# Two mixture-of-experts stages on Trainium2: the conditional blocks for overflowing tokens, two long ones per stage or six short ones

## The chip, the cores and the metric

The kernel runs on one core of one Trainium2 chip. The metric is the device time of one execution in microseconds (us). A core has five engines, each with its own list of instructions: PE (TensorE, the matrix products), DVE (VectorE), ACT (ScalarE), POOL (GpSimd) and SP (SyncE, which here issues the loads of the weights). An engine's sequencer (PEq, DVEq, ACTq, POOLq in the rows) walks the list, branches, and hands work to the engine; on PE it can be some microseconds ahead of the products. A conditional block is a compare-and-branch in the list of every engine that has work in the block: each reads the tested number into a register of its own and jumps over the block if the test fails.

## What is computed

A transformer of two layers on 256 tokens of width 1024, followed by further mixers and feed-forward stages. Each layer ends in a mixture of 16 experts of hidden width 512 in which every token takes two experts:

```python
D_MODEL = 1024
SEQ = 256
N_EXPERTS = 16
N_GROUPS = 4
TOP_K = 2
D_EXPERT = 512
# per token x and chosen expert e, with the gate weight cs[e]:
#   y += cs[e] * ((silu(x @ exp_w_gate[e]) * (x @ exp_w_up[e])) @ exp_w_down[e])
```

All three expert matrices are f32, 2 MB each, so that one layer's experts are 96 MB. How many tokens choose an expert is known only at run time.

## The kernel before, in words

An expert stage (`moe`, called once in each layer) takes the 16 experts in eight pairs, p = 0 to 7. The two experts of a pair sit side by side in the columns of PE. Each expert has 64 **places**: the tokens that chose it are brought into its places, pass through the three matrices, and are added back to their rows. For one pair PE runs, in this order:

- `up`: 16 rows of products for the gate (`pg`) and 16 for the up matrix (`pu`, both line 1486), out of `hg`, the pair's gathered tokens.
- the scatter that the pair before left over: products `py` (lines 1527 and 1528), whose sum DVE adds to `x` (line 1530); between its two halves stand four transposes `hT` (line 184) of the hidden values, for which ACT's silu and DVE's product are waited for.
- eight transposes `hgT` (line 184), which make the next pair's columns out of rows that POOL gathered (`rows`, line 1426, into the buffers `xh` and `xl`).
- `down`: 16 rows of products `po` (line 1540), whose result becomes `eo`, which is scattered in the next pair.

Where an expert has more than 64 tokens, two conditional blocks serve 32 further places each: `more_up` (line 1680) ahead of `pg`, and `more_down` (line 1683) ahead of `po`, in every pair from the third on. What the places don't hold goes through `rest` (lines 1620 to 1675): a block under `If(left > 96)` (line 1627) that takes all 128 tokens of one half of the sequence through one expert after the other, with its own loads of the weights on POOL's queue into `xh` and `xl`. `rest` stands twice in a stage, in the sixth pair (p = 5, first half of the tokens) and in the seventh (p = 6, second half), between `pu` and the silu; each block holds 16 shares, one for each expert. `left` is the largest count of the stage, with 32 added for the first two pairs, which have no further places. With the given inputs no count goes above 96, so that all engines jump over the block; `more_up` and `more_down` are run in some pairs and jumped over in others.

The weights come in 12 transfers of 1 MB for each pair, issued by SP into a ring of 18 slots: a slot is free again when the products of an earlier pair have read it. The order of instructions on an engine is the order of the code, within which a scheduler can move those that aren't pinned. [...] One row of f32 products in the lists below is four instructions (two weight loads and two products), one transpose is two.

## Time and profile before

| | us |
|---|---|
| median of three runs | 1566.06 |
| lowest and highest of the three | 1565.14 to 1566.18 |
| the profiled execution's own time | 1567.53 |
| its span in the trace | 1565.7 |
| PE busy in it | 1480.8 (95%) |
| DVE busy | 918.6 (59%) |
| ACT busy | 674.0 (43%) |

The span runs from the first to the last instruction of the profiled execution, and that execution's own time is 1.8 us more than its span. All times of the rows are counted from the span's start; the first expert stage lies at about 216 to 444, the second at about 604 to 821. A busy PE says only that a product was under way: a wait for a weight, for a branch or for another engine shows as idle time between products, and it is these that the rows are about.

### The profile page before, as it was taken

To read this page: it belongs to the slowest core of one execution; us is meant where nothing else is said; L and a number is where in the kernel's file an instruction comes from. 1 tells how busy PE (TensorE), PEld (TensorE's weight loads), DVE (VectorE), ACT (ScalarE), POOL (GpSimd) and SP (SyncE) were. 2 spreads that over 40 slices of the span, in tenths; PEclk is the share of its full clock that TensorE was granted. 3 is DMA by queue.
4 is the path that set the end of the run, shared out by engine and by line. 5 is a ranking of instruction groups with operands and counts; after the bars stand their busy time and mean duration, and the time that the engine had idled before them with its cause. 6 is when DMAs were issued, how large, how long until landed. Compare 5 with 4: busy or idle time off the path is not lost. (4 is left out here: it accounts for less than half of the span.)

```text
span 1565.7 us, 22964 instructions
## 1 busy us (share of the span) xinstructions
PE 1480.8 (95%) x8719; PEld 1046.1 (67%) x8719; DVE 918.6 (59%) x1800; ACT 674.0 (43%) x1404; POOL 141.2 (9%) x192
## 2 busy tenths in 40 slices
PE   6999999999989998999888999899999999999998
PEld 3666653334369974343336887788887997788886
DVE  3756453233269975332237867766667786766666
ACT  3444341111145543111016456655556565665554
POOL 0321011000000001000003001200001211110000
PEclk9999999999989999999999999999999999999999
DMA  9998999999967989999987531745463543546540
GB/s 357 335 316 302 348 420 417 421 418 418 376 215 246 318 326 413 419 420 419 418 362 235 159 120 65 239 143 197 163 211 121 182 135 97 193 143 212 190 161 27
DMA packets 172510, 418.13 MB, mean 267 GB/s; under 512 B 10376, under 2 KB 94016, under 8 KB 147792
## 3 DMA queue, kind: packets, MB, share of 16 engines
q1 hardware_dynamic: 165696, 403.46, 69.5%
q0 software_dynamic: 6400, 12.78, 2.5%
q8 instruction: 88, 1.44, 0.4%
q14 instruction: 54, 0.44, 0.1%
q10 hardware_dynamic: 272, 0.00, 0.0%
HBM read 422.13 MB, written 3.19 MB: 272 GB/s over the span
## 5 line engine op out<-in xcount | busy, mean ns | idle before, releaser
L230 DVE TENSOR_TENSOR hl<-w,hl 128x1024 fp32r<-128x1024 f32 x280 | 336.5, 1234 | 51.7 <-ACT hl L229 51.6
L229 ACT CAST hl<-w 128x1024 fp32r<-128x1024 f32 x280 | 280.3, 1046 | 32.0 <-DMA w<-in_even_w_in 19.0
L2350 PE MATMUL pgu<-hT,hl 128*128 128x512 f32 x640 | 224.4, 393 | 0.0
L2351 PE MATMUL pgu<-hT,hl 128*128 128x256 f32 x640 | 178.0, 279 | 0.0
L381 PE MATMUL lin<-hl,hThi 128*128 128x256 f32 (+2 forms) x480 | 159.3, 335 | 2.0 <-ACT hl L229 1.3
L382 PE MATMUL lin<-hl,hThi 128*128 128x256 f32 (+2 forms) x480 | 153.9, 321 | 2.0 <-DVE hl L230 1.7
L383 PE MATMUL lin<-hl,hTlo 128*128 128x256 f32 (+2 forms) x480 | 153.0, 320 | 0.4 <-DVE hTlo L558 0.4
L2350 PEld LDWEIGHTS pgu<-hT,hl 128*128 128x128 f32 x640 | 119.9, 187 | 27.1
L2351 PEld LDWEIGHTS pgu<-hT,hl 128*128 128x128 f32 x640 | 120.5, 188 | 2.0
L1540 PE MATMUL po<-w,hidT 128*64 128x512 f32 x512 | 114.6, 600 | 4.6 <-DVE x L1530 2.1
L1500 DVE TENSOR_TENSOR hd<-hd,pu 128x512 f32<-128x512 f32 x16 | 11.0, 687 | 183.8 <-PE pu L1486 183.8
L1486 PE MATMUL pg<-w,hg 128*64 128x512 f32 x512 | 113.7, 595 | 3.9 <-PEq L1680 3.6
L1486 PE MATMUL pu<-w,hg 128*64 128x512 f32 x512 | 115.0, 593 | 1.1 <-DMA w<-in_exp_w_up 1.1
L381 PEld LDWEIGHTS lin<-hl,hThi 128*128 128x128 f32 x480 | 92.9, 194 | 17.4 <-issue 8.1
L382 PEld LDWEIGHTS lin<-hl,hThi 128*128 128x128 f32 x480 | 92.9, 194 | 11.2 <-DVE hl L230 3.8
L383 PEld LDWEIGHTS lin<-hl,hTlo 128*128 128x128 f32 x480 | 92.6, 193 | 7.8 <-issue 1.7
L1486 PEld LDWEIGHTS pu<-w,hg 128*64 128x64 f32 x512 | 42.3, 137 | 70.8 <-issue 64.3
L1486 PEld LDWEIGHTS pg<-w,hg 128*64 128x64 f32 x512 | 40.1, 137 | 73.6 <-issue 57.7
L1540 PEld LDWEIGHTS po<-w,hidT 128*64 128x64 f32 x512 | 37.6, 138 | 71.4 <-issue 63.3
L1555 ACT CAST eo<-of 128x512 fp32r<-128x512 f32 x32 | 19.8, 618 | 130.4 <-DVE of L1552 130.1
L381 PE MATMUL linc<-hThi,hl 128*128 128x256 f32 x224 | 66.2, 296 | 0.0
L1443 ACT ACTIVATE hg<-hgT,ab 128x128 f32<-128x128 f32 x48 | 18.1, 457 | 111.0 <-PE hgT L184 111.0
(571 smaller groups left out, 2866.2 us busy)
## 6 DMA issues: line engine op xcount, KB each, us to landing
w<-in_exp_w_gate SPq DMA_DIRECT2D x64, 1024.0 KB
w<-in_exp_w_down SPq DMA_DIRECT2D x64, 1024.0 KB
w<-in_exp_w_up SPq DMA_DIRECT2D x64, 1024.0 KB
w<-in_ada_w SPq DMA_DIRECT2D x48, 1024.0 KB
w<-in_ffn_wg SPq DMA_DIRECT2D x22, 1024.0 KB
w<-in_ffn_wu SPq DMA_DIRECT2D x22, 1024.0 KB
w<-in_ffn_wd SPq DMA_DIRECT2D x22, 1024.0 KB
w<-in_even_w_in SPq DMA_DIRECT2D x14, 1024.0 KB
```

The lines of the kernel that those rows point to most:

```text
L229: pin(self.nc.scalar.copy(w[:, 0], src))
L230: pin(self.nc.vector.tensor_tensor(w[:, 1], src, w[:, 0].bitcast(F32), op=ALU.subtract))
L381: pin(mm(out, lh, rh, start=start, stop=False))
L382: pin(mm(out, lh, rl, start=False, stop=False))
L383: pin(mm(out, ll, rh, start=False, stop=stop))
L1443: nc.scalar.activation(out[:, k, :], pt[:, k, :], AF.Identity, scale=self.ab[:, 0, b, k:k + 1], bias=self.ab[:, 1, b, k:k + 1])
L1486: pin(mm(pp[64 * j:64 * j + 64, :], hg[0][:, p % 2, k, 64 * j:64 * j + 64], w[j][k // 4][:, k % 4, :], start=k == 0, stop=k == KD - 1, til ...
L1500: V.tensor_tensor(hd, hd, pu, op=ALU.mult)
L1540: pin(mm(po[c][64 * j:64 * j + 64, :], hidT[:, k, 64 * j:64 * j + 64], W[2][j][k // 2][:, k % 2, 512 * c:512 * c + 512], start=k == 0, sto ...
L1555: nc.scalar.copy(eh[c], of)
L2350: mm(pp[i], wh[:, k, :], both[:, :, k, :], start=k == 0, stop=False)
L2351: mm(pp[i][:, 0, :], wl[:, k, :], hi[:, k, :], start=False, stop=k == KD - 1)
```

## The change

`rest` becomes one block of five or six shares in every pair from the third to the eighth, instead of sixteen shares in each of two pairs: 6, 6, 5, 5, 5 and 5 shares in p = 2 to 7, in the order first half of the tokens, then second half. The number `left` is read into the engines' registers once in a stage and kept, instead of once for each block, and the copy that puts it where it can be read (`count_of(0)`) moves from p = 3 to p = 0. The weights' mask `wv`, the fetch of the half's rows and their columns are made again in each block (twice in the one that holds shares of both halves). In the changed kernel the `If` of `rest` stands on line 1633, its reading on line 1630, `more_up` on 1687 and `more_down` on 1690.

```diff
                 if FIRST <= p + 1 < 8:
                     count_of(p + 1)
-                if p == 3:
+                if p == 0:
                     count_of(0)
...
-            def rest(p, t):
-
-
-                left = nc.values_load(number_of[0][0:1, 0:1], min_val=0, max_val=2 * S,
-                                      engines=engines + (mybir.EngineType.Pool,))
-                with tc.If(left > 96):
+            left = []
+            shares = deque((t, e) for t in range(2) for e in range(NE))
+
+            def rest(p):
+
+
+
+                if not left:
+                    left.append(nc.values_load(number_of[0][0:1, 0:1], min_val=0, max_val=2 * S,
+                                               engines=engines + (mybir.EngineType.Pool,)))
+                mine = [shares.popleft() for _ in range(6 if p < 4 else 5)]
+                with tc.If(left[0] > 96):
...
-                    V.tensor_scalar(wv[:, 0:2 * FIRST], rk[:, t, 0:2 * FIRST], 64.0, None, op0=ALU.is_gt)
-                    V.tensor_scalar(wv[:, 2 * FIRST:], rk[:, t, 2 * FIRST:], 96.0, None, op0=ALU.is_gt)
-                    V.tensor_tensor(wv, wv, cs[:, t, :], op=ALU.mult)
-                    nc.gpsimd.dma_start(space[0][:, 0:D], xd[128 * t:128 * t + 128, 0:D])
-                    columns(space[0][:, 0:D], P, hc, banks[0:2])
...
-                    for e in range(NE):
+                    for q, (t, e) in enumerate(mine):
+                        if q == 0 or t != mine[q - 1][0]:
+                            V.tensor_scalar(wv[:, 0:2 * FIRST], rk[:, t, 0:2 * FIRST], 64.0, None, op0=ALU.is_gt)
+                            V.tensor_scalar(wv[:, 2 * FIRST:], rk[:, t, 2 * FIRST:], 96.0, None, op0=ALU.is_gt)
+                            V.tensor_tensor(wv, wv, cs[:, t, :], op=ALU.mult)
+                            nc.gpsimd.dma_start(space[n % 2][:, 0:D], xd[128 * t:128 * t + 128, 0:D])
+                            columns(space[n % 2][:, 0:D], P, hc, banks[0:2])
...
-                own = up(p, W, (lambda: rest(p, p - 5)) if p in (5, 6) else None)
+                own = up(p, W, lambda: rest(p))
```

The first place is PE's list in the third pair of the first layer (p = 2), as the difference between the two kernels; `be` are the block's own products, `hg` the gathered tokens.

```order
 L1486 MATMUL pg<-w,hg 64x512 x16
 L1486 MATMUL pu<-w,hg 64x512 x16
+L1633 COMPARE_AND_BRANCH
+L184 MATMUL be<-kt,xh 128x128 x8
+L1656 MATMUL be<-xl,hg 128x512 x4
+L1656 MATMUL be<-xh,hg 128x512 x4
...
+L1633 UNCONDITIONAL_BRANCH x2
 L1527 MATMUL py<-eo,kept 128x512
 L1528 MATMUL py<-eo,kept 128x512
```

Where `pu` was followed by the scatter of the pair before, a branch now stands between them, and behind it 6 shares of 24 rows of products and 4 transposes each, which the branch jumps over. In p = 3 to 6 of both layers the branch stands in the same way, right behind `pu`.

The second place is PE's list in the last pair (p = 7) of the first layer, in the changed kernel. Before, `pg` x16, `pu` x16 and the first `py` followed each other there without a branch.

```order
 L1486 MATMUL pg<-w,hg 64x512 x16
 L1486 MATMUL pu<-w,hg 64x512
 L1633 COMPARE_AND_BRANCH
 L184 MATMUL be<-kt,xh 128x128 x8
 L1656 MATMUL be<-xl,hg 128x512 x4
 L1656 MATMUL be<-xh,hg 128x512 x4
...
 L1633 UNCONDITIONAL_BRANCH x2
 L1486 MATMUL pu<-w,hg 64x512 x15
 L1527 MATMUL py<-eo,kept 128x512
 L1528 MATMUL py<-eo,kept 128x512
```

Here the scheduler puts the branch behind the first row of `pu`, and fifteen rows of `pu` come after the jump.

The third place is the first pair (p = 0), as the difference; `ph` are the products that gather the pair's tokens.

```order
 L1380 MATMUL ph<-kept,xh 128x256
 L1380 MATMUL ph<-kept,xl 128x256
+L1630 TENSOR_LOAD cnti_2005
+L1630 ISA x2
 L1486 MATMUL pg<-w,hg 64x512 x8
 L1380 MATMUL ph<-kept,xh 128x256
```

PE's reading of `left` moves from the pairs with a block to a place ahead of the first pair's first product.

## Rows read from the trace of the kernel before

**Rows 1.** Windows: the two stages; span, busy (count) by engine, PEclk, DMA share, GB/s.

```profile
216.00:444.00 228.00, 215.11 (x1075) 90.35 (x1074) 67.86 (x124) 34.24 (x84) 12.12 (x12) 0.98 0.96 395
604.00:821.00 217.00, 202.15 (x959) 86.80 (x958) 63.71 (x117) 31.74 (x75) 13.62 (x14) 0.98 0.99 409
```

**Rows 2.** Timeline, PE, first stage, pairs 4-6: start, duration, what, [idle, releaser].

```profile
345.49 7.07 PE L1486 MATMUL pu<-w,hg 128*64 128x512 f32 x32
...
356.39 7.09 PE L1540 MATMUL po<-w,hidT 128*64 128x512 f32 x32 [0.35 <-DVE x L1530]
...
370.70 7.07 PE L1486 MATMUL pu<-w,hg 128*64 128x512 f32 x32
379.72 0.59 PE L1527 MATMUL py<-eo,kept 128*128 128x512 f32 x1 [1.95 <-PEq L1627]
...
385.62 7.09 PE L1540 MATMUL po<-w,hidT 128*64 128x512 f32 x32 [0.83 <-DVEq L1683]
...
399.90 7.06 PE L1486 MATMUL pu<-w,hg 128*64 128x512 f32 x32
...
412.52 7.09 PE L1540 MATMUL po<-w,hidT 128*64 128x512 f32 x32 [0.34 <-DVE x L1530]
```

**Rows 3.** PE waits, 340 to 440: who for what, us, times, longest.

```profile
PE py L1527 <- PEq L1627: 3.6, 2, 2.0
...
PE po L1540 <- DVEq L1683: 0.8, 1, 0.8
```

**Rows 4.** Timeline of PE, second expert stage, pairs 5 and 6.

```profile
737.98 8.16 PE L1486 MATMUL pu<-w,hg 128*64 128x512 f32 x32
...
754.03 7.09 PE L1540 MATMUL po<-w,hidT 128*64 128x512 f32 x32 [0.30 <-DVEq L1683]
...
773.82 3.65 PE L1486 MATMUL pu<-w,hg 128*64 128x512 f32 x14 [1.05 <-DMA w<-in_exp_w_up]
...
785.79 0.39 PE L1528 MATMUL py<-eo,kept 128*128 128x512 f32 x1 [3.59 <-issue]
...
788.99 7.33 PE L1540 MATMUL po<-w,hidT 128*64 128x512 f32 x32 [0.30 <-DMA w<-in_exp_w_up]
```

**Rows 5.** Waits of PE from 640 to 822.

```profile
PE py L1527 <- PEq L1627: 5.4, 2, 2.8
...
PE pu L1486 <- DMA w<-in_exp_w_up: 1.1, 1, 1.1
```

**Rows 6.** Line 1627: operation, count, ns least/median/most, first, last start.

```profile
L1627 POOLq EVENT_SEMAPHORE  x16: 17/43/7722, 357.2 to 755.2; - x16
...
L1627 POOLq INC_SWDGE_SEM  x4: 746/924/1116, 365.2 to 757.4; - x4
...
L1627 PEldq COMPARE_BRANCH  x4: 5838/5977/6113, 373.3 to 773.9; - x4
```

**Rows 7.** Line 1627 from 372 to 374.

```profile
L1627 PEldq COMPARE_BRANCH  x1: 6102/6102/6102, 373.3 to 373.3; - x1
```

**Rows 8.** Line 1683, whole span.

```profile
L1683 PEldq COMPARE_BRANCH  x13: 71/238/4750, 282.0 to 811.6; - x13
```

**Rows 9.** Line 1680, whole span.

```profile
L1680 PEldq COMPARE_BRANCH  x13: 70/325/2725, 262.4 to 791.9; - x13
```

**Rows 10.** Line 1683 from 380 to 386.

```profile
L1683 PEldq COMPARE_BRANCH  x1: 4750/4750/4750, 380.6 to 380.6; - x1
```

**Rows 11.** DMA queues from 448.5 to 600: packets, MB, share.

```profile
q8 instruction: 9, 0.15, 0.4%
```

**Rows 12.** Windows: stretch of eight of those packets, without a branch.

```profile
448.57:590.45 141.88, 137.49 (x1019) 122.13 (x1019) 123.71 (x204) 81.97 (x154) 7.08 (x9) 0.95 0.83 290
```

**Rows 13.** Page: DMA queues of the whole span.

```profile
q8 instruction: 88, 1.44, 0.4%
```

**Rows 14.** Windows: behind one of PE idle stretches.

```profile
379.90:383.40 3.50, 3.50 (x11) 2.80 (x11) 2.13 (x4) 0.00 (x0) 0.98 (x1) 0.51 1.00 414
```

**Rows 15.** Line 1678: the loads of a count into a register.

```profile
L1678 PEldq TENSOR_LOAD <-cnti x12: 297/302/502, 252.0 to 645.8; - x12
```

## The prediction

> **What bounds the kernel now.** First the windows over the two expert stages [rows 1]: PE is busy for 215.11 of 228 us and for 202.15 of 217, and the DMA share is 0.96 and 0.99. Two resources are near their limit, so the reader has to find out which one ends last, and where. That is read from PE's waits. From 340 to 440 the view has five lines, none of them a transfer; the largest is PE's own sequencer at line 1627, 3.6 us in two waits [rows 3]. In the first stage the weights are there when PE wants them, and whatever PE loses there is lost to the end. From 640 to 822 the largest is the same, 5.4 us in two, but a weight is waited for too, 1.1 us [rows 5], and the `pu` of p = 5 takes 8.16 us [rows 4] where 7.07 is its length in the first stage [rows 2]: there PE has caught up with the transfers, and a loss ahead of that point is first paid out of these two waits, 1.1 + 1.1.

> The jump is partly hidden, because the sequencer is ahead of the products: it begins at 373.3 [rows 7], when `pu` still runs to 377.77 [rows 2], 4.5 us later. Of the 6.1 us, 1.95 show as idle time ahead of the first `py` [rows 2].

> The price of a block is therefore more than that wait. I take the time from the end of `pu` to the start of `po`, which holds the same work in every pair: 3.83 us at p = 4, without a block. With one it is 7.85 at p = 5 and 5.56 at p = 6 [rows 2], in the second stage 7.89 and 11.52 [rows 4]. The prices: 4.0, 1.7, 4.05 and 7.7. [...] Behind the jump of p = 5 the short jump of line 1683 took 4.75 us instead of 0.24 [rows 10], since after landing only the packet at the target is there, and the next one is asked for late. At the last of the four the landing is 18 instructions ahead of a packet's edge, and PE stands a second time, 3.59 us at 785.79 [rows 4]. [...]

> [...]

> **The change part by part.** It removes two far jumps of each stage, 4.0 + 1.7 = 5.7 us in the first and 4.05 + 7.7 = 11.75 in the second.

> It adds six jumps a stage. Five shares are 520 instructions and one half's columns 16, with the semaphore work about 555; with two halves 571, with six shares 659. All are over two packets of 256, so each lands outside of what is held, and costs the sequencer the 5.84 to 6.11 us of the old ones; that a jump is a third as long buys nothing. How much shows depends on where it lands. I counted packet edges in the built list in steps of 256, fixed by the stall at 785.79. With (A) an edge 136 to 147 instructions behind the landing, or right ahead of it, the jump over `more_down`, which itself lands 127 behind, stays in the packet, and only the first stall is left: between 1.7 and 4.05, the prices without a further stall and with half clock; I take 2.9. With (B) the edge 78 to 116 behind, that jump goes into a packet not yet there: 4.0 as at p = 5, bounds 1.7 and 5.1 (plus the weight wait's 1.1). With (C) the edge ten behind: a double stall like 785.79's, 7.7, bounds 6.8 and 8.4, that is 0.8 either way for the clock.

> - First stage: p = 2 is C, p = 3 A, p = 4, 5 and 6 B. At p = 7 the branch stands after one row of `pu`; the sequencer's lead over `pg` is as long as elsewhere, the first stall shows ahead of `pu`'s second row, and the next edge is hidden by fifteen rows (6.6 us): between 1.7 and 3.4, I take 2.5, since no half clock was seen to stretch `pu`. Sum 7.7 + 2.9 + 4.0 x 3 + 2.5 = 25.1, less 5.7: **+19.4**.
> - Second stage: p = 2 and p = 3 are A, p = 4 to 6 B, p = 7 as above: 5.8 + 12.0 + 2.5 = 20.3, less 11.75, less the two weight waits of 2.1 that a later PE no longer meets: **+6.5**.
> - PE's reading of `left` now stands ahead of the first pair's `pg`, behind DVE's copy: 0.30 us in the median of such readings and 0.50 at the longest [rows 15], once in each of two stages. If it falls into the sequencer's lead it costs 0, if all of it shows 1.0; the lead of 4.5 us is there elsewhere, so I take a value near the lower end, **+0.3**. The readings that vanish from the later pairs were in that lead and give nothing.
> - DVE, ACT and POOL jump too; POOL waits for its gathers' landing (7.7 us at the longest) and adds 0.75 to 1.1 [rows 6], now in each pair. Its increments at 365.2 came 8 us ahead of PE's jump at 373.3 [rows 6, 7]: nothing, as long as that lead holds.
> - The weights: no transfer is added while the block isn't taken; a later PE frees slots later, which only matters in the second stage, accounted for above.

> Sum 19.4 + 6.5 + 0.3 = +26.2. The profiled span of 1565.7 becomes about 1592; the profiled execution's own 1567.53 is 1.5 above the median of 1566.06, and the sum is put on the median: **1592**. A measurement of this kernel tells about 0.2%, 3.1 us, from no change.

> **Rivals.**
> (a) The shorter jumps hit what is already held, as a window wider than 660 instructions would have it. Each then costs the 0.24 to 0.33 of the short ones [rows 8, 9], hidden by the lead. The first stage gains 5.7 less six small waits of 0.3, or 3.9; the second, whose `pu` waits for weights already [rows 5], between 0 and 11.75 - 1.8 = 9.9, of which a third is taken, 3.4: about 1559, faster. For it: no jump between 150 and 1,700 instructions is in the trace. Against: a stall at 785.79 at a packet's edge would not be there if more than two were held. [...]
> (b) The jumps cost what I say, and the weights set the time anyway: DMA share 0.96 [rows 1]. Then PE's idle time merges with waits for weights and the sum is 0 to 3: 1566 to 1569. Against: no transfer among the waits of the first stage [rows 3].
> (c) PE's lateness frees slots later, the queue runs dry and a weight is late as well: one more wait of the length of one `pu`, 7.07 [rows 2], with the 1.1 of the weight wait that was there: some 8, about 1600.
> (d) POOL, in every pair now, becomes late: 7.7 + 1.1 = 8.8 us [rows 6] against a lead of 8, about 1 us for which `hgT` waits in each of five pairs of two stages, together 10: about 1602. Against: the 7.7 is the longest of 16, and runs while PE does its products.

> **How the numbers follow.** Forecast 0.66, (a) 0.08, (b) 0.08, (c) 0.10, (d) 0.08. With three A at 1.7 instead of 2.9, both p = 7 hidden and one B per stage at 1.7 the forecast falls by 13, to 1579, and a little below if the clock helps; with A at 4.05, B at 5.1 it rises by 3.5 + 6.6 + 1.8 to 1604, and with (c) or (d) a little more: the range is 1577 to 1608, which leaves out (a), (b) and the tails. Faster is (a), 0.08; same 0.06 and slower 0.02 out of (b), and all the rest slower: 0.86.

> **What would show it.** Six far jumps of 5.8 to 6.1 us in each stage at line 1633; 1.7 to 2.9 us of idle PE ahead of the first `py` in p = 2 to 6 and inside `pu` at p = 7; a second stall at line 1690 in p = 4 to 6; two stalls in p = 2 of the first stage; the first window longer by 19, the second by 6 to 7; no transfer among PE's waits of the second stage. Wrong it would be if the jumps of line 1633 took under a microsecond, or if PE's waits for weights grew by as much as those for its sequencer fell.

## The result and the profile after

The changed kernel takes 1592.58 us in the median of five executions (1589.92 to 1597.39), the kernel before 1566.06 beside it (1564.73 to 1567.34): a ratio of 1.0169, 95% interval 1.015 to 1.0188. It is slower by 26.5 us; 26.2 and 1592 were forecast. The span grew by 22.4 (1565.7 to 1588.1); the profiled execution, 1589.92, is the fastest of the five and lies 2.7 below their median, and that of before lies 1.5 above its own. The rows below are of these two executions and their 22.4 us; the 4.1 us by which the medians differ more stand in no trace.

The windows of the two stages, in the changed kernel, from the first `pg` to the last scatter of each:

```profile
214.30:455.90 241.60, 214.58 (x1073) 95.15 (x1073) 69.02 (x125) 34.34 (x86) 12.03 (x13) 0.98 0.92 375
617.10:843.60 226.50, 205.09 (x958) 88.48 (x958) 61.74 (x112) 30.49 (x73) 12.58 (x13) 0.97 0.95 389
```

Against [rows 1] PE does the same work within longer stretches, and the DMA share has fallen, from 0.96 to 0.92 and from 0.99 to 0.95: the weights are not what PE waits for. Its waits, the longest of the first stage and of the second:

```profile
PE py L1527 <- PEq L1633: 9.3, 5, 2.1
PE hT L184 <- issue: 4.6, 1, 4.6
...
PE po L1540 <- PEq L1690: 2.9, 3, 2.3
```

```profile
PE py L1527 <- PEq L1633: 9.8, 5, 2.1
PE po L1540 <- DMA w<-in_exp_w_up: 6.9, 3, 2.3
...
PE pu L1486 <- PEq L1633: 1.0, 1, 1.0
```

Two waits for its sequencer in a stage have become five, ahead of the first `py`, and in the second stage one more inside the last pair's `pu`. In the first stage the waits of `po` for line 1690 are new; the 6.9 us that the second stage's list puts down to a weight are taken up below. The jumps themselves, by line (1633 is `rest`, 1690 `more_down`):

```profile
L1633 PEldq COMPARE_BRANCH  x12: 3612/6115/6213, 274.8 to 820.3; - x12
```

```profile
L1690 PEldq COMPARE_BRANCH  x13: 82/450/4989, 287.2 to 834.5; - x13
```

Twelve far jumps with a median of 6.1 us, where there were four of 5.98 [rows 6]; one took 3.6. Of the thirteen at line 1690 six took 4.79 to 4.99 us: those of p = 4, 5 and 6 in both stages (4.79, 4.92 and 4.90; 4.99, 4.98 and 4.88). They are the six landings that the prediction had as B, and the seven others took under half a microsecond.

The double stall in p = 2 of the first stage is in PE's timeline:

```profile
272.21 7.07 PE L1486 MATMUL pu<-w,hg 128*64 128x512 f32 x32
281.19 0.48 PE L1527 MATMUL py<-eo,kept 128*128 128x512 f32 x1 [1.91 <-PEq L1633]
...
286.95 1.13 PE L184 MATMUL hT<-kt,hd 128*128 128x128 f32 x4 [4.58 <-issue]
...
291.07 7.09 PE L1540 MATMUL po<-w,hidT 128*64 128x512 f32 x32 [0.30 <-PEq L1690]
```

After the landing four products run, then PE stands again, for 4.58 us, with no releaser named ("issue"), as at 785.79 before [rows 4]. From the end of `pu` to `po` it takes 11.79 us.

That PE's sequencer waits for a fetch at these places can be read from the times of the packets in the queue q8, "instruction" in the view, in the same trace. That PE's list comes through it shows in the kernel before: over the eight packets of [rows 12] the trace has 1019 products, 1019 weight loads and ten semaphore instructions of PE, which gives 256 for each packet of 16 KB. Behind the start of each of the eleven far jumps that took 5.8 us or more the next packet begins after 3.36 to 3.76 us and takes 1.0 to 1.1 us, and the jump ends 1.3 to 1.5 us after it; behind the start of the six long jumps at line 1690 it begins after 2.4 to 2.5 us. At the jump of p = 2 it begins at 278.32; from 278.3 to 279.4 the view of the queues has

```profile
q8 instruction: 1, 0.02, 5.8%
```

The second stall ends in the same way: the packet behind it begins at 284.39 and takes 1.07 us, and PE goes on 1.5 us later, at 286.95. In all fourteen traces together PE has 111 jumps of over 1 us, and each of them ends 1.3 to 1.6 us after the end of such a packet.

One reading has to be made with care. In p = 4 of the second stage the timeline and the list of waits put `po` down to a weight:

```profile
731.89 7.07 PE L1486 MATMUL pu<-w,hg 128*64 128x512 f32 x32
741.02 0.47 PE L1527 MATMUL py<-eo,kept 128*128 128x512 f32 x1 [2.06 <-PEq L1633]
...
743.44 1.11 PE L184 MATMUL hgT<-kt,xh 128*128 128x128 f32 x8
746.89 8.78 PE L1540 MATMUL po<-w,hidT 128*64 128x512 f32 x32 [2.34 <-DMA w<-in_exp_w_up]
```

```profile
L1690 PEldq COMPARE_BRANCH  x1: 4989/4989/4989, 741.6 to 741.6; - x1
```

The sequencer is inside the jump of line 1690 from 741.58 for 4.99 us, to 746.57, and `po` begins at 746.89. The transfer that the view names is one of the up matrix, which `po` does not read, and it has landed only 21.4 us after its issue, at 748.8, when `po` is already running:

```profile
L222 SPq DMA_DIRECT2D w<-in_exp_w_up x1: 328/328/328, 727.4 to 727.4; - x1
...
  PE po L1540: 2.3, 1
...
DMA to landing us min/median/max: 21.4/21.4/21.4
```

The last of the four transfers of the down matrix that `po` does read here landed at 736.3. So the branch is what ended last, not the weight, and the two other waits of this kind, in p = 5 and 6, end in the same way, 0.3 us behind a jump of line 1690. And `po` takes 8.78 us in place of 7.09, at a granted clock of 0.59 from 746.50 to 750.00:

```profile
746.50:750.00 3.50, 3.11 (x8) 1.14 (x10) 0.04 (x1) 0.00 (x0) 0.00 (x0) 0.59 1.04 409
```

### The profile page after: what moved, and what is told of

Its sections match the earlier page's. It is cut to its first block, busy times and chain, and to the rows that moved or that the text cites. A ratio compares the mean times of both kernels' runs of the same rounds, so it can differ in the third digit from the quotient of the medians.

```text
span 1588.1 us, 23110 instructions
## 1 busy us (share of the span) xinstructions
PE 1482.1 (93%) x8719; PEld 1051.2 (66%) x8719; DVE 918.9 (58%) x1800; ACT 673.4 (42%) x1404; POOL 140.7 (9%) x192
## 5 line engine op out<-in xcount | busy, mean ns | idle before, releaser
L1540 PE MATMUL po<-w,hidT 128*64 128x512 f32 x512 | 119.1, 617 | 14.8 <-DMA w<-in_exp_w_up 6.9
L1540 PEld LDWEIGHTS po<-w,hidT 128*64 128x64 f32 x512 | 41.2, 141 | 82.1 <-issue 65.2
L1552 DVE SCALAR_TENSOR_TENSOR of<-po,ws,gate 128x512 f32<-128x512 f32 x32 | 23.9, 748 | 81.8 <-PE po L1540 81.8
```

The lines of the kernel that those rows point to most:

```text
L1540: pin(mm(po[c][64 * j:64 * j + 64, :], hidT[:, k, 64 * j:64 * j + 64], W[2][j][k // 2][:, k % 2, 512 * c:512 * c + 512], start=k == 0, sto ...
L1552: V.scalar_tensor_tensor(of, po[c], ws, gate[:, cs], op0=ALU.mult, op1=ALU.mult)
```

## The experiments

Times are medians; each is compared with executions of the kernel before on the same chip, whose median was 1568.36 us for the kernels with no block, two shares, no products of PE and the early count, 1566.40 for the two splits and the first two early blocks, and 1567.26 for the thin block, the two early blocks with the counts placed, and four shares.

**No block at all.**

```diff
-                own = up(p, W, (lambda: rest(p, p - 5)) if p in (5, 6) else None)
+                own = up(p, W)
```

> The kernel before without either block of rest, so that tokens beyond the places would not be served (there are none with these inputs). Fetch theory (the price of a block is PE's far jump, 5.7 us in the first stage and 11.75 in the second before, of which the second stage's weights give back only a part): 1557 us, 1554 to 1560. If the weights set the time of both stages anyway: 1563 to 1566. Either way this is the floor against which all prices are read.

1561.89 us, ratio 0.9945 (0.9928 to 0.9962): 6.5 us less than before, where 9 were expected; the time lies in neither of the two ranges. The second stage's waits are now for weights:

```profile
PE pu L1486 <- DMA w<-in_exp_w_up: 7.7, 6, 1.3
```

This is the floor: without any jump the first stage is 5.6 us shorter (222.03 against 227.63 from the first `pg` to the last scatter), the second only 1.7 (214.34 against 216.06), since `pu` now waits 7.7 us for weights there, where before it waited 1.1 [rows 5].

**Two shares in a block.**

```diff
-                mine = [shares.popleft() for _ in range(6 if p < 4 else 5)]
+                mine = [shares.popleft() for _ in range(2)]
```

> The changed kernel with two shares in each of the six blocks, 236 instructions of PE instead of 553 to 660; twenty shares are left out. Fetch theory: a jump of less than one packet lands in the packet held or in the next one, already fetched; 1558 us, up to 1566 if one or two lands too early; the jumps under 1 us. Per-block theory (DVE's, ACT's and POOL's jumps, POOL's wait for its gathers, semaphores): as the changed kernel, 1588 to 1595. Length theory (a jump's price in proportion to what it skips): 1571.

1561.41 us, ratio 0.9951 (0.9935 to 0.9967), as the floor.

```profile
L1633 PEldq COMPARE_BRANCH  x12: 313/325/3620, 275.2 to 793.4; - x12
```

Two of the twelve took 3.62 and 1.87 us and show in no wait, the longest at this line being 0.3 us; ten took 0.31 to 0.44. Six conditional blocks whose jump is short cost 2.8 us in the first stage (224.81 against 222.03), and in the second the waits of `pu` for weights are 5.9 us in five, in place of the floor's 7.7 in six.

**Blocks without PE's part, and with a thin one.** In the first a share's products are left out of the code, in the second all but two rows of them and the four transposes, so that the result is not computed; the loads and the work on DVE, ACT and POOL stay. A part of the second's edit:

```diff
-                                for k in range(4):
-                                    mm(banks[2 + i], hc[:, 4 * b + k, :], w[:, k, :], start=b + k == 0, stop=b + k == 4)
+                                if b == 0 and i == 0:
+                                    mm(banks[2], hc[:, 0, :], w[:, 0, :], start=True, stop=True)
...
```

> The changed kernel's six blocks with the same numbers of shares, their loads and their work on DVE, ACT and POOL, but without any product or transpose of PE (a share computes nothing useful), so that PE has nothing to jump over. Fetch theory: 1557 to 1562, no wait of PE at the block's line. Per-block theory: 1585 to 1593, since DVE, ACT and POOL still branch in every pair.

1573.84 us, ratio 1.0042 (1.0027 to 1.0056): neither number. PE's jumps took 0.2 to 0.32 us, but a new wait appeared, here in the first stage:

```profile
PE hT L184 <- DVE hd L1500: 10.5, 6, 2.5
```

With nothing of PE in the block, the scheduler put one of the scatter's adds ahead of it on DVE and another ahead of silu's product, so that `hT` came late. The run can't tell the theories apart, and the thin version, where DVE's order is that of the changed kernel, was made for that:

> The changed kernel's six blocks with all their shares, loads and work on DVE, ACT and POOL, in the changed kernel's order, but with PE's part of a share cut to two rows of products and four transposes (a share computes nothing useful): PE jumps over 107 to 126 instructions in place of 553 to 660. Fetch theory: 1561 us, 1557 to 1566, PE's jumps under 1 us but for one that may meet an edge. Per-block theory (the other engines' jumps and waits): 1585 to 1593. Unlike the block without PE work, the scatter's adds on DVE keep their place behind the block.

1560.75 us, ratio 0.996 (0.9946 to 0.9974), the floor again.

```profile
L1633 PEldq COMPARE_BRANCH  x12: 202/268/418, 275.8 to 793.8; - x12
```

DVE, ACT and POOL branch as often as in the changed kernel, twelve times each at this line, and POOL waits as it does there, 9.1 us at the longest against 8.9; the 32 us between the two kernels hang on how many of PE's instructions the jump passes, 107 to 126 or 553 to 660. This run also has what a block costs without a long jump. From `pu` to `po` it takes 4.18 us in p = 5 of the first stage where 3.85 are the floor, 0.33 more. In the last pair of the first stage, where the block stands inside `pu`, PE pauses although the jump took 0.42 us:

```profile
421.81 1.02 PE L1486 MATMUL pu<-w,hg 128*64 128x512 f32 x2
422.99 7.05 PE L1486 MATMUL pu<-w,hg 128*64 128x512 f32 x30
```

The two products before the block end at 422.83, and the third starts at 422.99 instead of beside them. Behind the block the list has an event on line 1633 that waits for PE's own count of finished work, and it runs only then, 4.9 us after the end of the jump:

```profile
L1633 PEldq EVENT_SEMAPHORE  x1: 51/51/51, 422.9 to 422.9; - x1
```

So here PE's sequencer waited until the products ahead of it were through. The pair is 1.2 us longer than the floor's.

**Where the landing lies.** Two other splits of the same 32 shares; the second stands in the same place, as `(6, 4, 6, 7, 4, 5)[p - 2]`.

```diff
-                mine = [shares.popleft() for _ in range(6 if p < 4 else 5)]
+                mine = [shares.popleft() for _ in range((4, 5, 5, 5, 7, 6)[p - 2])]
```

> The changed kernel with 4, 5, 5, 5, 7 and 6 shares in the blocks instead of 6, 6, 5, 5, 5 and 5: the same 32 shares, six jumps and nearly the same list, but by the count of the list every landing has 136 to 222 instructions to the next packet's edge (125 in the very last). Landing theory (the second stall at more_down's jump, or right behind the landing, falls away, and with it the half clock behind it): 1578 us, 1574 to 1584. If only the number of far jumps counts: 1592.

> The same with 6, 4, 6, 7, 4 and 5 shares: in each stage two landings have 10 to 16 instructions to the edge (a double stall of some 8 us each), two have 103 to 108, one 239 or 243. Landing theory: 1606 us, 1599 to 1612. If only the number of far jumps counts: 1592.

1576.76 us, ratio 1.0065 (1.0043 to 1.0088), and 1602.18, ratio 1.0217 (1.0196 to 1.0238): 25 us apart, with six far jumps in each stage of both. The jumps of line 1690 in the two:

```profile
L1690 PEldq COMPARE_BRANCH  x13: 82/243/446, 283.1 to 824.4; - x13
```

```profile
L1690 PEldq COMPARE_BRANCH  x13: 82/341/4839, 287.9 to 850.2; - x13
```

In the first, whose landings by the count of the list have 125 to 222 instructions to an edge, none takes over 0.45 us. In the other split the four landings that the count puts 10 to 16 instructions ahead of an edge have a second stall of 3 to 4 us each, and from `pu` to `po` 11.6 to 12.4 us; three of the four at 103 to 108 have a jump at line 1690 of 4.7 to 4.8 us, and the fourth, at p = 3 of the first stage, has none, since `more_down` is run there.

**The block earlier in `up`.** The first kernel has the six blocks of the changed one, the second all 32 shares in the block of p = 2 and no other.

```diff
                     for k in range(KD):
+                        if between and w is W[1] and k == 1:
+                            between()
...
-                if between:
-                    between()
```

> The changed kernel's six blocks, the same shares, but each placed behind the second row of the pair's pu, with fourteen rows of pu after it, about where the last pair's block stands already (its price there was 1.15 us in the first stage and 2.04 in the second, where 3.6 to 8 were paid elsewhere). Fetch theory with what follows the landing hidden by those rows: 1565 us, 1560 to 1571. If a far jump costs the same wherever it stands: 1592.

> One block of all 32 shares in the third pair, behind the second row of pu: one far jump of 3,433 instructions in a stage. Fetch theory: the floor (the kernel without blocks) plus some 1 to 3 us, 1558 us, 1555 to 1562, faster than both kernels. Length theory: two jumps of twice the length cost what four did, 1566 or more.

1590.99 us, ratio 1.0147 (1.0126 to 1.0168), and 1574.64, ratio 1.0045 (1.0027 to 1.0062): both missed, by 26 and 17 us. The first is the very time of the other theory, that a far jump costs the same wherever it stands. But the waits at the block are short, 9.2 us for six in the first stage and 12.0 in the second, and PE lost time ahead of the first pair, 6.1 and 7.5 us. In the second stage:

```profile
PE pu L1488 <- PEq L1633: 12.0, 6, 3.8
PE pg L1488 <- DVE cnti L1346: 7.5, 1, 7.5
```

In the list of both kernels the scheduler had moved PE's reading of five pairs' counts ahead of the first pair's `pg`, each behind a copy that DVE makes between other work. With the copies placed right at the block's new place the reads stand behind that pair's products again, once more with six blocks and with one:

```diff
+                        if w is W[1] and k == 1:
+                            if FIRST <= p + 1 < 8:
+                                count_of(p + 1)
+                            if p == 0:
+                                count_of(0)
+                            if between:
+                                between()
...
-                if FIRST <= p + 1 < 8:
-                    count_of(p + 1)
-                if p == 0:
-                    count_of(0)
```

> The early blocks again (behind the second row of pu), with the copies of the counts placed so that PE reads the six pairs' counts behind the first pair's products, as in the changed kernel, and not ahead of them. If the 6.1 and 7.5 us ahead of the first pair came of those reads: they are gone, and 12 jumps at about 2.0 us each over the floor, less what the second stage's weights hide, give 1573 us, 1568 to 1577. If the early place itself brought them: 1591.

> One block of 32 shares in the third pair, behind the second row of pu, with the counts placed likewise. One jump of about 2 us in the first stage, one in the second that the weights hide: 1560 us, 1557 to 1564, faster than both kernels. If a longer jump costs more: 1566 or more.

1573.22 us, ratio 1.0044 (1.0031 to 1.0057), and 1557.77, ratio 0.994 (0.9925 to 0.9955). Of the first, and of the second:

```profile
PE pu L1493 <- PEq L1634: 21.7, 12, 4.5
```

```profile
PE pu L1493 <- DMA w<-in_exp_w_up: 5.7, 5, 1.3
...
PE pu L1493 <- PEq L1634: 3.7, 2, 1.9
```

Twelve far jumps cost 21.7 us of waiting there, the pause behind the block included, two cost 3.7, and the kernel with one block in a stage is faster than both kernels, by 0.6% than the one before, although its jump passes 3,433 instructions:

```profile
L1634 PEldq COMPARE_BRANCH  x2: 6146/6168/6191, 269.8 to 650.4; - x2
```

So what the first two early kernels lost came in the main of the reads of the counts, and not of the place of the block.

**Equal lengths, different packets.** The same edit as for two shares, with `range(4)`.

> The changed kernel with four shares in each block (eight left out): every jump skips 447 to 449 instructions, but by the count of the list three land in the packet behind the one they start from (p = 3 of the first stage, p = 2 and 7 of the second) and nine in the one after that. Two packets held: those three take some 0.3 us, the nine 5.8 to 6.2. If the length decides: all twelve alike. Total between the kernel with two shares and the changed one, about 1580 us, 1572 to 1590.

1573.38 us, ratio 1.0048 (1.0033 to 1.0063). The three landings in the next packet:

```profile
L1633 PEldq COMPARE_BRANCH  x1: 3660/3660/3660, 315.9 to 315.9; - x1
```

```profile
L1633 PEldq COMPARE_BRANCH  x1: 2632/2632/2632, 670.3 to 670.3; - x1
```

```profile
L1633 PEldq COMPARE_BRANCH  x1: 5982/5982/5982, 802.5 to 802.5; - x1
```

The 0.3 us is missed: 3.66, 2.63 and 5.98. Of the nine others eight took 5.80 to 6.20 us, and one, in the first stage's last pair, 3.85. By the count of the list these three jumps start 5, 15 and 8 instructions behind an edge, so the packet that they go to is at best on its way: in q8 it begins 1.2 and 0.2 us after the start of the first two, and 3.5 us after that of the third, as behind a far jump. In the run with two shares one of the ten quick jumps stays in its packet and the others start 49 or more instructions into it; the two slow ones start 54 and 22 in, and their packets begin 1.1 us after the start of the jump and 0.6 before it. Neither the length nor the count alone tells the quick from the slow; when the packet comes does. The prediction's reading, that the sequencer holds the packet it is in and the next one, held in these runs only once the next one had come.

**The early count alone.**

```diff
-                if p == 3:
+                if p == 0:
                     count_of(0)
...
+                if not lefts:
+                    lefts.append(nc.values_load(number_of[0][0:1, 0:1], min_val=0, max_val=2 * S,
+                                                engines=engines + (mybir.EngineType.Pool,)))
+                with tc.If(lefts[0] > 96):
```

> The kernel before, with only the copy of the largest count moved to the first pair and its number read once in a stage, the two long blocks unchanged. Prediction's term: 1566.4, the +0.3 within the error. Rival (the reading ahead of the first pair holds PE up, behind DVE's copy): 1568 to 1570.

1564.57 us, ratio 0.9975 (0.9959 to 0.9991): a small gain, which neither number had. The first pair takes 25.53 us from `pg` to `pg` in both stages, as before. In the profiled execution p = 2 of the first stage is 1.5 us shorter (36.40 against 37.86), and the products `pgu` ahead of the next `pg` take 7.07 us in place of 8.53; whether that is the whole gain was not settled.

## Why the prediction came out

The price by pairs, from one `pg` to the next (the last pair to the end of its `po`); the floor is the kernel without blocks where PE sets the pace:

| | p = 2 | 3 | 4 | 5 | 6 | 7 | sum over the floor | forecast |
|---|---|---|---|---|---|---|---|---|
| first stage, floor | 37.89 | 33.62 | 25.22 | 25.23 | 25.20 | 23.89 | | |
| before | 37.86 | 33.60 | 25.22 | 29.19 | 26.91 | 23.88 | 5.6 | 5.7 |
| after | 44.28 | 34.15 | 28.77 | 29.47 | 28.85 | 25.04 | 19.5 | 25.1 |
| second stage, before | 25.22 | 25.23 | 25.22 | 30.33 | 35.20 | 23.88 | 15.1 | 13.85 |
| after | 28.75 | 28.02 | 30.98 | 30.86 | 30.77 | 25.93 | 25.3 | 20.3 |

(In the second stage the floor is 25.22 and 23.88: without blocks its later pairs wait for weights.)

- **The far jump pays wherever it stands, and a shorter one buys nothing.** Right: 5.8 to 6.2 us in eleven of twelve, and the packet that each waits for is in the trace. The thin block shows that it is PE's list and not the other engines' branches, and the single long block that more length adds nothing: 6.15 and 6.19 us for 3,433 instructions.
- **The landing decides the price.** Right in kind, in every pair: double stall at p = 2, the second jump in the six B's, none in the A's; the two splits show it as a cause, 25 us apart.
- **The sizes.** The sum held, 44.8 us against 45.4, because two errors cancel, and that is luck: the first stage grew by 13.9 us, not by the 19 that the prediction gave as a sign, and the second by 10.2, not by 6 to 7. (Together that is 24.1 us, where the span grew by 22.4: the first `pg` starts 1.8 us earlier, at 214.37 in place of 216.17, for which there is no term and no explanation.) The first stage was put 5.6 us too high. The jump of p = 2 cost 7.95 from `pu` to `po`, as sized, but the pair got back 1.6 in `more_up`, whose products ran at a granted clock of 1.00 from 301.09 to 308.16 and took 7.07 us, where before they took 8.53, at 0.57 in their first 3.50 us:

```profile
295.02 8.53 PE L1575 MATMUL pgu<-w,hga 128*32 128x512 f32 x64 [1.90 <-ACT hga L1443]
```

```profile
301.09 7.07 PE L1575 MATMUL pgu<-w,hga 128*32 128x512 f32 x64 [1.84 <-ACT hga L1443]
```

That gift does not belong to the landing: the run with the early count has it without a block in that pair, and the second split, with the same double stall there, has not (46.16 us from `pg` to `pg`). In p = 3, sized at 2.9, the stall of 1.99 is there, but `po` took 7.09 in place of the floor's 8.01 (before it took 8.00, with a granted clock of 0.50 from 328.70 to 332.10, and in the changed kernel it was 1.00 from 335.80 to 343.20), and the pair netted 0.5; in the first split the same pair cost 3.5. p = 7 cost 1.15 instead of 2.5: there the far jump was hidden altogether, and what is left is the pause behind the block that the thin version has too. The second stage was put 5.0 too low: the three B's, sized 4.0, cost 5.5 to 5.8, since behind each stall `po` took 8.78 us instead of 7.09, at a granted clock of 0.59, 0.52 and 0.51 in stretches of 3.5 us from 746.50, 777.75 and 808.52; their upper bound of 5.1 was too low. (The half clock of the prediction's bounds is that of [rows 14], 0.51.) The prediction priced a block by the time from `pu` to `po`, and what the clock gives and takes in the products outside of that stretch is in none of its terms: it makes up the whole error of the second stage, three times 1.69, and about half of that of the first, 1.46 and 0.92.

- **What the second stage gives back.** Put at 13.85 with the two weight waits, 15.1 in the profile; no `pu` waits for a weight in the changed kernel, as forecast.
- **The reading of `left`**, +0.3, is not seen; the early count by itself did not slow the kernel. That the term could have been 7.5 us in a stage is shown by the two early versions, where the scheduler put other reads in that place; the prediction's 1.0 was no bound on it.
- **The rivals.** Short jumps that hit: seen at 236 instructions, in ten of twelve, and refuted for 447 and more, none of which took under 2.6 us. Weights that hide all: refuted for the changed kernel, true in the second stage of the floor. Weights or POOL late: POOL is not among PE's waits, and the weights are only for 0.3 us in a stage, once the three waits of `po` are read as above.

## What to carry to other kernels

In this kernel a conditional block that is never taken was priced by how much of PE's list its jump passes (0.31 to 0.44 us for ten of twelve jumps over 236 instructions, 5.8 to 6.2 for eleven of twelve over 553 to 660) and by where it lands (25 us between the two splits), not by its contents: one long block in a stage was cheaper than six middling ones in the same place, 1557.77 us against 1573.22, and in the thin version, with jumps of at most 0.42 us, a block cost 0.33 us between two groups of products and 1.2 inside one. So look for a place for a far jump where work with no dependence on it follows at once: with fourteen rows of `pu` behind it, and the counts placed, the six blocks came to a ratio of 1.0044, where the changed kernel has 1.0169. And before believing a wait that a view puts down to a transfer, look at what the waiting engine's sequencer was doing at that time.

## What was not expected of the hardware

- The half clock came and went: behind long jumps at line 1690 the three `po` of the first stage took 7.09 us at a granted clock of 1.00, those of the second 8.78, at 0.59, 0.52 and 0.51 in the stretches above. What decides it was not settled.
- In the run with four shares the jumps that the count of the list puts into the very next packet were not free, starting 5 to 15 instructions behind an edge: 2.63 to 5.98 us.
- In the last pair of the first stage the far jump took 3.61 us in the changed kernel, 3.85 in two of the others and 6.18 in the first split. In the three short ones the packet begins 1.0 to 1.5 us after the start of the jump, in place of the 3.4 to 3.8 of the jumps of 5.8 us and more; my reading is that it had been asked for before the jump. Why there alone is open.
